# The first column pair of a SwiGLU block in seven products instead of eight, with the sum-free products of two pairs run first, fewer sum buffers, and the output projection in four parts instead of three

## The chip, the cores and the metric

The kernel runs on one core of a Trainium2 chip. The metric is the device time of one execution in microseconds (us). Before the change the median of three runs is 1446.42 us (1444.23 to 1446.85).

The engines are named as in the profile: PE (TensorE matmul; PEld its weight loads), DVE (VectorE), ACT (ScalarE), POOL (GpSimd) and SP, which only issues DMAs here. Each engine works through its own instruction queue in order. An instruction that has to wait for a semaphore holds up everything behind it on its engine.

## What is computed

Two layers of a hybrid decoder on 512 tokens of width 1024, in float32. Each layer has a token mixer, a cross-attention into 256 memory tokens and a SwiGLU feed-forward block, each followed by a residual and a LayerNorm. The change touches the feed-forward block:

```python
D_MODEL, SEQ, DEPTH, D_FF = 1024, 512, 2, 2816

def swiglu(x, w_in, w_out):
    g, u = jnp.split(x @ w_in, 2, axis=-1)
    return (jax.nn.silu(g) * u) @ w_out

def reference(...):
    h = layer_norm(x, ln0_g, ln0_b)
    for l in range(DEPTH):
        mix = hybrid_mixer(h, ...)
        h = layer_norm(DEEPNORM_ALPHA * h + mix, ln1_g[l], ln1_b[l])
        xa = memory_cross_attention(h, mem, ...)
        h = layer_norm(DEEPNORM_ALPHA * h + xa, ln2_g[l], ln2_b[l])
        ff = swiglu(h, w_ffn_in[l], w_ffn_out[l])
        h = layer_norm(DEEPNORM_ALPHA * h + ff, ln3_g[l], ln3_b[l])
    return h
```

## The kernel before

**Precision.** Every large product is made of three matmuls (`mm3`, lines 136 to 139): an operand is split into a rounded high part and the remainder, and high·high, high·low and low·high are added up in PSUM. The split (`split`, lines 100 to 102) is one copy on ACT (line 101, the high part) and one subtraction on DVE or POOL (line 102, the low part). A weight block of 128x1024 is loaded by SP into a staging buffer (`raw_...`, pool `stage`, 4 buffers), and its two halves are written into a ring of 4 slots (`w_...`, pool `ring`). A load waits until its staging buffer is free, and a split waits until its ring slot has been read for the last time by PE.

**The feed-forward block.** The 2816 gate columns and 2816 up columns are worked off in 11 pairs of column blocks (j = 0, 2, ... 20; each 256 columns of gate and 256 of up). The input x (tokens by features) is cut into four blocks: Bkt holds feature half k and token half t (B00, B10 of the first 256 tokens, B01, B11 of the last 256). A plain pair needs eight products of a 512x256 weight quarter by such a block. Ten of the eleven pairs use seven products (a scheme of Strassen's kind): some products take a sum of weight quarters, some take a sum of the blocks of x. A product is 24 matmuls of 128x256: 2 row blocks m, 4 slices k, 3 precision terms. So a plain pair is 192 matmuls (`swiglu_plain`, lines 348 to 371) and a pair in seven products 168 (`swiglu_seven`, lines 373 to 454).

**The sums of x.** T1 to T4, the sums of blocks, are made by `Quads` (lines 286 to 333). It is called as LN2, the LayerNorm ahead of the block, finishes each of the four 128-token tiles: PE transposes the tile (`lt_ln`, line 198), `take` (line 306) splits it into its Bkt block and updates the raw sums q11, q21 and q12. After tile 3, the last, `combine` (line 329) finishes T1 to T4, tile by tile. The first two products of a pair, on B00 and B10, need only tiles 0 and 1.

**The sums of weights.** A pair in seven products loads four quarters by SP: a11, a12, a22 into staging buffers and the fourth into s1, one of the quarter buffers (pool `quad`: 4 buffers, of which q11, q21, q12 take three while LN2 runs). DVE forms s3 = s1 + a11 and s2 = (s1 + a22) + a11 (lines 384 and 386), POOL issues two accumulating DMAs (`add_into`, line 284): s1 += a22, and later s2 += a12. Seven splits follow. A buffer that an accumulating DMA reads is free once that DMA has landed.

**Order.** The program's order per engine is set by a list scheduler at build time, from its own estimate of the durations. The plain pair j = 0 stands first: its 96 matmuls on B00 and B10 run while LN2 finishes tiles 2 and 3, and its 96 matmuls on B01 and B11 run while DVE and ACT make T1 to T4.

**The output projection** (`out_proj`, line 254) runs in three parts, after 4, 8 and 11 pairs (8, 8 and 6 row blocks of 128). Each part multiplies its row blocks by 128x1024 pieces of w_ffn_out, of which the first four take ring slots and the others `block` buffers, and adds the result to h by eight DVE instructions (line 273, two per token tile). In layer 0 the last part's tiles go straight into LN3, whose output is the input of layer 1's first projection (`pp_c`, weights `w_c`, split on ACT and POOL).

Of the kernel before, what the change touches and what calls it, by code (L numbers as in the profile page):

```python
# [20 lines left out]
P = 128  # L21
# [19 lines left out]
NBLK = 15  # L41
RAW = 4
TMP = 4
EVB = 6
# [7 lines left out]
def trunk(ctx: ExitStack, tc, a, out):  # L52
# [9 lines left out]
    quad = ctx.enter_context(tc.tile_pool(name="quad", bufs=4))  # L62
# [223 lines left out]
    class Quads:  # L286
# [4 lines left out]
        def __init__(self, name):  # L291
            self.name = name
            self.b = {(i, t): block([P, 2, 4, 256], F32R, f"B{i}{t}_{name}") for t in range(2) for i in range(2)}
            self.raw = {n: quarter([P, 4, 256], f"q{n}_{name}") for n in ("11", "21", "12")}
            self.d = {n: block([P, 2, 4, 256], F32R, f"{n}_{name}") for n in ("T3", "T1", "T2", "T4")}
            self.late = []

        def split_t(self, n, src, s, neg=False):
            hi, lo = self.d[n][:, 0, :, s], self.d[n][:, 1, :, s]
            if neg:  # L300
                ACT.activation(hi, src, AF.Copy, scale=-1.0)
                DVE.scalar_tensor_tensor(lo, src, -1.0, f(hi), ALU.mult, ALU.subtract)
            else:
                split(hi, lo, src)

        def take(self, i, tt, pv):
            s = slice((tt % 2) * P, (tt % 2 + 1) * P)
            b = self.b[i, tt // 2]
            r11, r21, r12 = (self.raw[n][:, :, s] for n in ("11", "21", "12"))
            split(b[:, 0, :, s], b[:, 1, :, s], pv)  # L310
            if tt < 2:
                ACT.activation((r11, r21)[i], pv, AF.Copy)
            elif i == 0:
                ACT.activation(r12, pv, AF.Copy)
                DVE.tensor_sub(r11, r11, pv)
                self.split_t("T1", r11, s)
            else:
                DVE.tensor_add(r11, r11, pv)
                DVE.tensor_sub(r12, pv, r12)

                def rest():
                    DVE.tensor_sub(r21, r11, r21)
                    self.split_t("T3", r12, s)
                    self.split_t("T2", r11, s, neg=True)
                    self.split_t("T4", r21, s)

                self.late.append(rest)
# [20 lines left out]
    def swiglu_plain(w, q, j, ph, pl, name):  # L348

        ws = [[split_quarter(load_quarter(w, kh, c0, f"g{c0}{kh}_{name}"), f"g{c0}{kh}_{name}") for kh in range(2)]  # L350
              for c0 in (j * P, DFF + j * P)]
        banks = [[bank(f"pp_f{j}{g}{m}_{name}") for m in range(2)] for g in range(2)]
        for t in range(2):
            for g in range(2):
                for kh in range(2):
                    for m in range(2):
                        ms = slice(m * P, (m + 1) * P)
                        for k in range(4):
                            mm3(banks[g][m][:, t * 256:(t + 1) * 256], ws[g][kh][:, 0, k, ms], ws[g][kh][:, 1, k, ms],
                                q.b[kh, t][:, 0, k, :], q.b[kh, t][:, 1, k, :],  # L360
                                kh == 0 and k == 0, kh == 1 and k == 3)
        out = []
        with tc.high_priority(offset=HP):
            for m in range(2):
                sg = tmp.tile([P, T], F32, tag="t", name=f"sg{j}{m}_{name}")
                ACT.activation(sg, banks[0][m], AF.Silu)
                DVE.tensor_mul(sg, sg, banks[1][m])
                split(ph[:, m, :], pl[:, m, :], sg)
                out.append((ph[:, m, :], pl[:, m, :]))
        return out  # L370

    def swiglu_seven(w, q, j, ph, pl, i0, name):
# [5 lines left out]
        s1, s2, s3 = (quarter([P, 1024], n(f"s{i}")) for i in range(1, 4))  # L378
        r11 = load_quarter(w, 0, cg, n("a11"))
        load_quarter(w, 0, cu, n("s1"), s1)  # L380
        r22 = load_quarter(w, 1, cu, n("a22"))
        r12 = load_quarter(w, 1, cg, n("a12"))
        w1 = split_quarter(r11, n("a11"))
        DVE.tensor_add(s3, s1, r11)
        add_into(s1, r22)
        DVE.tensor_add(s2, s1, r11)
        w7 = split_quarter(s3, n("s3"))
        w6 = split_quarter(s2, n("s2"))
        add_into(s2, r12)
        w2 = split_quarter(r12, n("a12"))  # L390
        w5 = split_quarter(s1, n("s1"))
        w3 = split_quarter(s2, n("s4"))
        w4 = split_quarter(r22, n("a22"))
        t3, t1, t2, t4 = q.t
# [23 lines left out]
        lo, hi = slice(0, 256), slice(256, 512)  # L418
# [4 lines left out]
        W = banks_of("fw", "cv")  # L423
        product(w7, t3, W, True, False)
# [3 lines left out]
        Y = banks_of("fy", "tr")  # L428
# [500 lines left out]
```

## Time and profile before

| | before |
|---|---|
| runs | 1444.23, 1446.42, 1446.85 us; median 1446.42 |
| the profiled execution | 1448.14 us, of which the span in the trace is 1446.4 |
| mean granted clock of PE | 0.992 |
| DMA | 168.62 MB, mean 117 GB/s |

The span is what the trace covers, from the first to the last instruction; 1.7 us of the profiled execution lie outside of it. In rows of the timeline the first two numbers are the start and the length in us, and what stands in brackets is the idle time of the engine just before and what ended it. A matmul row's length includes the way through the array, so the rate of matmuls is read from the distance of their starts. In rows of a window the columns are its length, then for each engine the busy time and the number of instructions, then the granted clock as a share of full speed, the DMA share and GB/s. The chain of waits lists what the end of a stretch hung on, piece by piece; a piece "DMA" is a transfer from its issue to its landing, and "issue" is time in which nothing is waited for that the profile shows.

### The profile page before, as it was taken

How to read it: one execution, taken by the hardware profiler on the slowest of the kernel's cores; microseconds unless marked ns; L12 is line 12 of the kernel's file. 1: busy time of each engine (PE TensorE's matmuls, PEld its weight loads, DVE VectorE, ACT ScalarE, POOL GpSimd, SP SyncE). 2: the span in 40 equal slices, each digit the busy share in tenths (PEclk: the TensorE clock that was granted, in tenths of full speed). 3: DMA queues.
4: the chain of work that ended last, by engine and by line, in shares of the span. 5: the costliest groups of instructions: out<-in, count | busy, mean ns of one | idle time of the engine just before them, and what ended most of it. 6: DMA issues, size and time to landing. Idle time of an engine off the chain costs nothing.

```text
span 1446.4 us, 22112 instructions
## 1 busy us (share of the span) xinstructions
PE 1405.3 (97%) x8943; PEld 1257.2 (87%) x8943; DVE 1015.9 (70%) x1674; ACT 608.8 (42%) x976; POOL 218.8 (15%) x124
## 2 busy tenths in 40 slices
PE   8999999999999999999979999999999999999997
PEld 7787878988999899899877888889889998998996
DVE  6699977557877367466859997685578664763767
ACT  5553362442555155245225335424424542561550
POOL 3467230000000000000133423300000000000000
PEclk9999999999999999999989999999999999999999
DMA  7423250221365265545242323612214662643641
GB/s 248 131 79 117 88 190 25 95 86 58 97 161 170 76 168 131 147 113 128 84 126 84 93 85 115 217 59 88 76 51 119 164 190 59 161 135 114 146 132 58
DMA packets 108730, 168.62 MB, mean 117 GB/s; under 512 B 7485, under 2 KB 81937, under 8 KB 108629
## 3 DMA queue, kind: packets, MB, share of 16 engines
q1 hardware_dynamic: 102548, 145.98, 32.1%
q0 software_dynamic: 5760, 20.97, 7.8%
q8 instruction: 70, 1.15, 0.3%
q14 instruction: 32, 0.25, 0.1%
q10 hardware_dynamic: 320, 0.27, 0.1%
HBM read 144.13 MB, written 2.10 MB: 101 GB/s over the span
## 4 chain that ended last, share of the span: by engine, by line
PE 76%; DVE 14%; DMA 5%; ACT 3%; issue 2%; POOL 0%; SPq 0%; DVEq 0%; POOLq 0%; ACTq 0%
DVE cv L590 6%; PE po_fo L137 5%; PE po_fo L138 5%; PE po_fo L139 5%; PE fx L402 5%; PE fx L404 5%; PE fx L403 5%; DMA s<-raw_a 3%; PE fw L404 2%; PE fw L403 2%; PE fw L402 2%; PE pp_xq L137 2%; PE pp_xq L138 2%; PE pp_xq L139 2%; PE po_mo L139 2%
## 5 line engine op out<-in xcount | busy, mean ns | idle before, releaser
L284 POOL DMA_DIRECT2D s<-raw_a x40 | 34.9, 885 | 873.4 <-DVE w_s L102 256.1
L590 DVE SCALAR_TENSOR_TENSOR cv<-u,chan,cv 128x511 f32<-128x511 f32 (+28 forms) x240 | 158.6, 728 | 0.3
L138 PE MATMUL po_fo<-w_fo,ph 128*128 128x512 f32 (+1 forms) x358 | 138.1, 386 | 0.0
L139 PE MATMUL po_fo<-w_fo,pl 128*128 128x512 f32 (+1 forms) x358 | 137.0, 386 | 0.0
L137 PE MATMUL po_fo<-w_fo,ph 128*128 128x512 f32 (+1 forms) x358 | 131.7, 386 | 0.0
L101 ACT ACTIVATE w_a<-raw_a 128x1024 fp32r<-128x1024 f32 x60 | 63.2, 1054 | 150.6 <-PE po_fo L139 124.6
L102 DVE TENSOR_TENSOR w_s<-s,w_s 128x1024 fp32r<-128x1024 f32 x80 | 97.3, 1220 | 33.3 <-ACT w_s L101 33.0
L101 ACT ACTIVATE w_s<-s 128x1024 fp32r<-128x1024 f32 x80 | 83.8, 1052 | 48.0 <-DMA s<-raw_a 27.6
L402 PE MATMUL fx<-T_ln,w_s 128*128 128x256 f32 x320 | 91.6, 287 | 3.5 <-ACT u L415 3.3
L403 PE MATMUL fx<-T_ln,w_s 128*128 128x256 f32 x320 | 91.2, 285 | 0.0
L404 PE MATMUL fx<-T_ln,w_s 128*128 128x256 f32 x320 | 90.6, 285 | 0.0
L273 DVE SCALAR_TENSOR_TENSOR h<-h,po_fo 128x512 f32<-128x512 f32 (+1 forms) x49 | 32.3, 671 | 71.2 <-PE po_fo L139 71.1
L102 DVE TENSOR_TENSOR w_a<-raw_a,w_a 128x1024 fp32r<-128x1024 f32 x60 | 73.0, 1220 | 9.1 <-ACT w_a L101 8.1
L139 PEld LDWEIGHTS po_fo<-w_fo,pl 128*128 128x128 f32 x358 | 67.3, 188 | 13.3
L138 PEld LDWEIGHTS po_fo<-w_fo,ph 128*128 128x128 f32 x358 | 67.3, 188 | 13.0
L137 PEld LDWEIGHTS po_fo<-w_fo,ph 128*128 128x128 f32 x358 | 66.9, 188 | 12.9
L402 PEld LDWEIGHTS fx<-T_ln,w_s 128*128 128x128 f32 x320 | 62.2, 194 | 4.2 <-ACT u L415 3.7
L102 DVE TENSOR_TENSOR w_fo<-raw_fo,w_fo 128x1024 fp32r<-128x1024 f32 x44 | 52.8, 1219 | 13.6 <-ACT w_fo L101 13.6
L403 PEld LDWEIGHTS fx<-T_ln,w_s 128*128 128x128 f32 x320 | 62.2, 194 | 0.0
L404 PEld LDWEIGHTS fx<-T_ln,w_s 128*128 128x128 f32 x320 | 61.8, 194 | 0.0
L138 PE MATMUL pp_xq<-hT_ln,w_xq 128*128 128x256 f32 (+1 forms) x192 | 61.3, 322 | 0.0
L139 PE MATMUL pp_xq<-hT_ln,w_xq 128*128 128x256 f32 (+1 forms) x192 | 60.3, 319 | 0.0
(315 smaller groups left out, 4478.3 us busy)
## 6 DMA issues: line engine op xcount, KB each, us to landing
raw_a<-w_ffn_in SPq DMA_DIRECT2D x60, 512.0 KB
raw_fo<-w_ffn_out SPq DMA_DIRECT2D x44, 512.0 KB
s<-raw_a POOLq DMA_DIRECT2D x40, 512.0 KB, 4.9
s<-w_ffn_in SPq DMA_DIRECT2D x20, 512.0 KB
raw_xk<-w_xkv SPq DMA_DIRECT2D x16, 512.0 KB
raw_c<-w_in SPq DMA_DIRECT2D x16, 512.0 KB
raw_xv<-w_xkv SPq DMA_DIRECT2D x16, 512.0 KB
raw_mo<-w_mix_out SPq DMA_DIRECT2D x16, 512.0 KB
```

The lines of the kernel that those rows point to most:

```text
L101: ACT.activation(hi, src, AF.Copy)
L102: eng.tensor_sub(lo, src, f(hi))
L137: PE.matmul(o, lh, rh, start=start, stop=False)
L138: PE.matmul(o, lh, rl, start=False, stop=False)
L139: PE.matmul(o, ll, rh, start=False, stop=stop)
L273: DVE.scalar_tensor_tensor(h[tt][:, c0:c1], h[tt][:, c0:c1], scale, bks[c][:, :c1 - c0], ALU.mult, ALU.add)
L284: POOL.dma_start(dst, src, accum_op=ALU.add)
L402: PE.matmul(o, wh, bh, start=start and k == 0, stop=False, skip_group_check=True)
L403: PE.matmul(o, wh, bl, start=False, stop=False, skip_group_check=True)
L404: PE.matmul(o, wl, bh, start=False, stop=stop and k == 3, skip_group_check=True)
L590: DVE.scalar_tensor_tensor(cv[ct][:, s:], u[:, ct, :T - s], wj, cv[ct][:, s:], ALU.mult, ALU.add)
```

## The change

`swiglu_plain` and `swiglu_seven` are replaced by one generator, `swiglu_pair`, for all 11 pairs. It first makes the two products that need no sum (X = a11·B00, Y = a12·B10) and then yields. For the first part of the output projection, pairs 0 and 2 are both started up to there, then `combine` is run, then the rest of pair 0 and of pair 2.

- The gate half of the first 256 tokens (`g`) is evicted right after Y into its own tile (pool `evp`, 6 to 8 buffers). Multiplying gate by up becomes four 128x256 DVE instructions per pair instead of two of 128x512.
- Weight sums are formed in place: a11 += s1 (DVE), s2 = a11 + a22 (DVE), s1 += a22 (POOL's accumulating DMA), a12 += s2 (another). Two quarter buffers per pair instead of three; the pools hold 5 quarters instead of 4, 5 staging buffers instead of 4, 14 blocks instead of 15.
- `Quads`: B01 is not stored any more. T1 is still made per tile; the three other sums are made in `combine` by whole 128x1024 instructions, after tile 3. They are now numbered T0 to T3 in the code: T0 is the old T2, T1 the old T3, T2 the old T1, T3 the old T4.
- The output projection has parts of 4, 6, 6 and 6 row blocks. In the last part of layer 0 only two of its weight pieces take ring slots.
- `reset`, a constant of the GLA scan, becomes a temporary tile that POOL fills in each layer.

```diff
-NBLK = 15
-RAW = 4
+NBLK = 14
+RAW = 5
-EVB = 6
+EVB = 8
...
-    quad = ctx.enter_context(tc.tile_pool(name="quad", bufs=4))
+    quad = ctx.enter_context(tc.tile_pool(name="quad", bufs=5))
...
-    def out_proj(w, stat, name, scale, norm=None, fin=False):
+    def out_proj(w, stat, name, scale, norm=None, fin=False, nring=RING):
-        wcs = [wchunk(w[k * P:(k + 1) * P, :], 1, D, f"{name}{k}", resident=k >= RING) for k in range(nk)]
+        wcs = [wchunk(w[k * P:(k + 1) * P, :], 1, D, f"{name}{k}", resident=k >= nring) for k in range(nk)]
...
         def combine(self):
-            for rest in self.late:
-                rest()
-            self.t = [self.d[n] for n in ("T3", "T1", "T2", "T4")]
+            t2, t4, t3 = (self.raw[n].rearrange("p k t -> p (k t)") for n in ("11", "21", "12"))
+            hi, lo = ([], [])
+            for i in (0, 1, 3):
+                d = self.new_t(i).rearrange("p j k t -> p j (k t)")
+                hi.append(d[:, 0])
+                lo.append(d[:, 1])
+            ACT.activation(hi[0], t2, AF.Copy, scale=-1.0)
+            DVE.scalar_tensor_tensor(lo[0], t2, -1.0, f(hi[0]), ALU.mult, ALU.subtract)
+            split(hi[1], lo[1], t3)
+            DVE.tensor_sub(t4, t2, t4)
+            split(hi[2], lo[2], t4)
...
-    def swiglu_plain(w, q, j, ph, pl, name):
...
-    def swiglu_seven(w, q, j, ph, pl, i0, name):
+    def swiglu_pair(w, q, j, pT, early, name):
...
+        r11 = load_quarter(w, 0, cg, n("a11"))
+        r12 = load_quarter(w, 1, cg, n("a12"))
+        w1 = split_quarter(r11, n("a11"))
+        w2 = split_quarter(r12, n("a12"))
         X = banks_of("fx", "acc")
         product(w1, q.b[0, 0], X, True, False)
         with tc.high_priority(offset=HP):
             x = copies("x")
+        Y = banks_of("fy", "cv" if early else "tr")
+        product(w2, q.b[1, 0], Y, True, True)
+        with tc.high_priority(offset=HP):
+            glo = two(evp, 256, "e", "g")
+            for m in range(2):
+                DVE.tensor_add(glo[m], Y[m][:, lo], x[m])
+                ACT.activation(glo[m], glo[m], AF.Silu)
+        yield
+        t2, t3, t1, t4 = q.t
+        s1, s2 = (quarter([P, 1024], n(f"s{i}")) for i in range(1, 3))
+        load_quarter(w, 0, cu, n("s1"), s1)
+        r22 = load_quarter(w, 1, cu, n("a22"))
+        DVE.tensor_add(r11, s1, r11)
+        DVE.tensor_add(s2, r11, r22)
+        add_into(s1, r22)
+        w6 = split_quarter(s2, n("s2"))
+        add_into(r12, s2)
+        w7 = split_quarter(r11, n("s3"))
+        w5 = split_quarter(s1, n("s1"))
+        w3 = split_quarter(r12, n("s4"))
+        w4 = split_quarter(r22, n("a22"))
         product(w6, t2, X, False, False)
...
-        quads.combine()
-        for part, (j0, nj) in enumerate(((0, 8), (8, 8), (16, 6))):
+        for part, (j0, nj) in enumerate(((0, 4), (4, 6), (10, 6), (16, 6))):
...
+            if part == 0:
+                next(pairs[0])
+                next(pairs[1])
+                quads.combine()
+            for pair in pairs:
+                for _ in pair:
+                    pass
```

In the built program PE has 48 matmuls fewer, DVE 68 instructions more, ACT 12 more, POOL 8 more, and SP as many as before. Three places show how the order moves. A name ends in numbers that only tell buffers apart; a line number of the program after is three less than the same helper's line before.

On DVE, at the end of LN2 in layer 0, `y_ln2_03` is the reciprocal deviation of tile 3, and `h3` is the tile itself, which PE transposes next. Before, the last steps stand between instructions on the blocks of x:

```order
L154 SCALAR_TENSOR_TENSOR t_ln2_03_3356<-y_ln2_03_3355,v_ln2_03_3351 128x1
L102 TENSOR_TENSOR T3_ln2_0_2982<-q12_ln2_0_2981,T3_ln2_0_2982 128x4x128
L159 SCALAR_TENSOR_TENSOR s_ln2_03_3357<-t_ln2_03_3356 128x1
L302 SCALAR_TENSOR_TENSOR T2_ln2_0_2984<-q11_ln2_0_2979,T2_ln2_0_2984 128x4x128
L160 SCALAR_TENSOR_TENSOR y_ln2_03_3355<-s_ln2_03_3357,y_ln2_03_3355 128x1
L102 TENSOR_TENSOR T4_ln2_0_2985<-q21_ln2_0_2980,T4_ln2_0_2985 128x4x128
L190 SCALAR_TENSOR_TENSOR h3_103<-h3_103,y_ln2_03_3355,gb_ln2_0_2972 128x512 x2
```

After the change the same place on DVE holds the weight sums and splits of pairs 0 and 2 (`raw_a112` is a11 of pair 2, `s12` its fourth quarter as loaded by SP, `s22` its s2):

```order
L99 TENSOR_TENSOR w_s20_0_3542<-s20_0_3535,w_s20_0_3542 128x1024
L99 TENSOR_TENSOR w_s10_0_3549<-s10_0_3534,w_s10_0_3549 128x1024
L99 TENSOR_TENSOR w_s40_0_3552<-raw_a120_0_3382,w_s40_0_3552 128x1024
L154 SCALAR_TENSOR_TENSOR y_ln2_03_3349<-t_ln2_03_3350,y_ln2_03_3349 128x1
L393 TENSOR_TENSOR raw_a112_0_3452<-s12_0_3706,raw_a112_0_3452 128x1024
L151 SCALAR_TENSOR_TENSOR t_ln2_03_3350<-y_ln2_03_3349,v_ln2_03_3345 128x1
L394 TENSOR_TENSOR s22_0_3707<-raw_a112_0_3452,raw_a222_0_3709 128x1024
L156 SCALAR_TENSOR_TENSOR s_ln2_03_3351<-t_ln2_03_3350 128x1
L157 SCALAR_TENSOR_TENSOR y_ln2_03_3349<-s_ln2_03_3351,y_ln2_03_3349 128x1
L187 SCALAR_TENSOR_TENSOR h3_100<-h3_100,y_ln2_03_3349,gb_ln2_0_2972 128x512 x2
```

The finishing of tile 3 now stands behind the sums of pair 2 (L393 and L394). The quarter buffer into which SP loads `s12` is that of `s20`, pair 0's s2; the load waits in SP's queue for POOL's accumulating DMA raw_a120 += s20, which reads `s20`, and for the split w_s20. Layer 1 has the same order.

On PE, around the transposes of tile 3 (`lt_ln2_03`), before:

```order
L139 MATMUL pp_f011_0_3425<-B10_ln2_0_2976,w_g28161_0_3419 128x256
L198 MATMUL lt_ln2_03_0_3365<-ident_85,h3_103 128x128 x4
L198 MATMUL lt_ln2_03_1_3377<-ident_85,h3_103 128x128 x4
L137 MATMUL pp_f000_0_3422<-B01_ln2_0_2977,w_g00_0_3404 128x256
L137 MATMUL pp_f001_0_3423<-B01_ln2_0_2977,w_g00_0_3404 128x256
```

The same place on PE after:

```order
L359 MATMUL fy12_0_3493<-B10_ln2_0_2976,w_a122_0_3459 128x256
L195 MATMUL lt_ln2_03_0_3359<-ident_85,h3_100 128x128 x4
L195 MATMUL lt_ln2_03_1_3369<-ident_85,h3_100 128x128 x4
L357 MATMUL fx00_0_3390<-T0_ln2_0_3524,w_s20_0_3542 128x256
L357 MATMUL fx10_0_3391<-T0_ln2_0_3524,w_s20_0_3542 128x256
```

In both, 96 matmuls on B00 and B10 stand ahead of the transposes. Behind them came matmuls on B01, a copy of the transposed tile; now come matmuls on T0, a sum made by `combine`.

On ACT, at the end of layer 0, `w_c0_100` to `w_c0_111` are the first four weight pieces of layer 1's first projection, and `hT00_ln3` is the split of LN3's transposed tiles. Before:

```order
L101 ACTIVATE hT00_ln3_0_6547<-lt_ln3_00_0_6640 128x4x128
L101 ACTIVATE hT01_ln3_0_6548<-lt_ln3_00_1_6648 128x4x128
L101 ACTIVATE w_c0_100_6903<-raw_c0_100_6901 128x1024
L101 ACTIVATE w_c0_101_6908<-raw_c0_101_6906 128x1024
L101 ACTIVATE w_c0_110_6915<-raw_c0_110_6913 128x1024
L101 ACTIVATE hT00_ln3_0_6547<-lt_ln3_01_0_6714 128x4x128
L101 ACTIVATE hT01_ln3_0_6548<-lt_ln3_01_1_6722 128x4x128
L101 ACTIVATE w_c0_111_6920<-raw_c0_111_6918 128x1024
```

The same place on ACT after:

```order
L98 ACTIVATE w_c0_100_6954<-raw_c0_100_6952 128x1024
L98 ACTIVATE w_c0_101_6959<-raw_c0_101_6957 128x1024
L98 ACTIVATE wa_1_7281<-wa_raw_1_7273 128x8x16
L578 ACTIVATE w2_555<-wa_raw_1_7273 96x256
L98 ACTIVATE hT00_ln3_0_6598<-lt_ln3_00_0_6691 128x4x128
L98 ACTIVATE hT01_ln3_0_6599<-lt_ln3_00_1_6699 128x4x128
L98 ACTIVATE w_c0_110_6966<-raw_c0_110_6964 128x1024
L98 ACTIVATE w_c0_111_6971<-raw_c0_111_6969 128x1024
```

The first two pieces now stand ahead of LN3's first tile, since their ring slots are those of the last pair's weights and no longer those of the output projection. POOL makes the low halves of all four in the same sequence, and each waits for its ACT copy. The other two still wait for the last token tile of the output projection.

More of the change, by code (lines that the diff above doesn't have):

```diff
@@ L346, in split_quarter @@
         return w
[L348 to L372 removed]
+    def swiglu_pair(w, q, j, pT, early, name):
         n = lambda s: f"{s}{j}_{name}"
         cg, cu = j * P, DFF + j * P
[L378 to L394, printed above, removed]
+        lo, hi = slice(0, 256), slice(256, 512)
         def product(wq, b, banks, start, stop):
```

75 lines of the change are left out of this document (28 added, 47 removed).

## The prediction

> **What bounds the kernel now.** I began with the busy time of each engine and the chain that ended last (sections 1 and 4 of the page).
>
> ```profile
> PE 1405.3 (97%) x8943; PEld 1257.2 (87%) x8943; DVE 1015.9 (70%) x1674; ACT 608.8 (42%) x976; POOL 218.8 (15%) x124
> PE 76%; DVE 14%; DMA 5%; ACT 3%; issue 2%; POOL 0%; SPq 0%; DVEq 0%; POOLq 0%; ACTq 0%
> ```
>
> PE is busy for 97% of the span, so a matmul taken away is time gained, and a new hole in PE is time lost. Hence the question at each place: does PE still have something to do? The timeline of the end of LN2 in layer 0 (first five rows), and of the first stall behind it in each layer:
>
> ```profile
> 371.13 0.28 PE L137 MATMUL pp_f<-B_ln,w_g 128*128 128x256 f32 x1
> 371.25 0.28 PE L138 MATMUL pp_f<-B_ln,w_g 128*128 128x256 f32 x1
> ...
> 382.52 0.29 PE L139 MATMUL pp_f<-B_ln,w_g 128*128 128x256 f32 x1
> 382.65 1.04 PE L198 MATMUL lt_ln<-ident,h 128*128 128x128 f32 x8
> 383.93 0.74 PE L137 MATMUL pp_f<-B_ln,w_g 128*128 128x256 f32 x4 [0.25 <-ACT B_ln L101]
> ...
> 430.48 0.39 PE L402 MATMUL fx<-T_ln,w_s 128*128 128x256 f32 x1 [1.50 <-ACT u L415]
> ...
> 1145.31 0.39 PE L402 MATMUL fx<-T_ln,w_s 128*128 128x256 f32 x1 [1.82 <-ACT u L415]
> ```
>
> Matmuls of 128x256 start 0.12 us apart. The 96 on B00 and B10 run from 371.13 to 382.65; exactly then tile 3's transposes start, and 0.25 us after them PE goes on with the plain pair. The same end of LN2 on DVE, and how a DVE queue looks when it does wait for an accumulating DMA, 18 us later:
>
> ```profile
> 381.24 1.40 DVE L190 SCALAR_TENSOR_TENSOR h<-h,y_ln,gb_ln 128x512 f32<-128x512 f32 x2
> ...
> 399.43 1.23 DVE L386 TENSOR_TENSOR s<-s,raw_a 128x1024 f32<-128x1024 f32 x1 [1.71 <-DMA s<-raw_a]
> ```
>
> Tile 3 is finished at 381.24 plus 0.7 (its first half), in step with PE.
>
> **The change part by part.** The windows give what PE loses now in the stretches that change: the starts of both feed-forward blocks (rows 1 and 4) and the passage between the layers (rows 2 and 3).
>
> ```profile
> 383.00:436.00 53.00, 50.73 (x411) 49.35 (x410) 40.33 (x50) 30.58 (x49) 4.50 (x5) 1.00 0.56 137
> 712.00:732.00 20.00, 11.97 (x60) 9.64 (x59) 19.90 (x28) 6.19 (x8) 9.36 (x4) 0.86 0.31 76
> 732.00:760.00 28.00, 28.00 (x219) 27.58 (x218) 10.02 (x24) 9.43 (x14) 7.21 (x3) 0.92 0.37 118
> 1097.50:1150.00 52.50, 49.97 (x392) 48.57 (x390) 39.22 (x48) 29.18 (x47) 4.37 (x5) 0.97 0.55 133
> ```
>
> *Removed.* 24 matmuls per layer at 0.12: 2.9 us each. PE idles 53.00 - 50.73 = 2.3 us at layer 0's start, and at layer 1's 52.50 - 49.97 = 2.5 plus 0.03 x 52.5 = 1.6 of lowered clock, 4.1. These small holes belong to the old order; I count all of them as gone, which favours the change.
>
> *New wait ahead of tile 3.* This is the largest term. Tile 3's last DVE steps now stand behind a11 += s1 and s2 = a11 + a22 of pair 2. These need the quarter s12, which SP can load only once POOL's accumulating DMA has read pair 0's s2. So an accumulating DMA and a load, one after the other, stand between pair 0's s2 and the transposes. The pieces of the chain of waits price them:
>
> ```profile
> 394.15 0.54 issue
> ...
> 394.71 4.70 DMA s<-raw_a
> ...
> 404.74 6.11 DMA s<-raw_a
> 414.79 6.46 DMA raw_a<-w_ffn_in
> ...
> 1086.82 6.58 DMA s<-w_ffn_in
> 1108.90 4.63 DMA s<-raw_a
> 1129.29 4.77 DMA raw_a<-w_ffn_in
> 1135.44 8.40 DMA s<-raw_a
> ```
>
> The groups give the sums and splits (mean ns of one behind the busy time), and three timeline rows the smaller steps:
>
> ```profile
> L102 DVE TENSOR_TENSOR w_s<-s,w_s 128x1024 fp32r<-128x1024 f32 x80 | 97.3, 1220 | 33.3 <-ACT w_s L101 33.0
> L386 DVE TENSOR_TENSOR s<-s,raw_a 128x1024 f32<-128x1024 f32 x20 | 24.4, 1222 | 47.2 <-DMA s<-raw_a 47.2
> L101 ACT ACTIVATE w_s<-s 128x1024 fp32r<-128x1024 f32 x80 | 83.8, 1052 | 48.0 <-DMA s<-raw_a 27.6
> ...
> 368.53 3.48 DVE L102 TENSOR_TENSOR w_g<-raw_g,w_g 128x1024 fp32r<-128x1024 f32 x3
> ...
> 383.28 1.08 ACT L101 ACTIVATE B_ln<-lt_ln 128x512 fp32r<-128x512 f32 x2 [3.00 <-PE lt_ln L198]
> ...
> 431.33 0.42 DVE L433 TENSOR_TENSOR sg<-fy,x 128x256 f32<-128x256 f32 x1
> ```
>
> When is pair 0's s2 ready? At 371.13 PE starts the early products as before. DVE ends its splits of early weights near 372, as it does now (368.53 + 3.48), and has then six steps of tile width (0.6 to 0.7 each, the row at 381.24 halved), one sum of 1.2, a 128x256 step of 0.4 and less than 0.1 of small ones; with s2 itself some 377.8 if each starts a little before the one ahead of it ends, as such rows do. Then 0.5 us to issue, the accumulating DMA 4.6 to 6.1 (once 8.4), the load 4.8 to 6.6, two sums at 1.2, four small steps and half of tile 3, 3.4 together. That gives 391.1 to 394.4; with 8.4 for the DMA 396.7. PE has run out at 382.65. The middle, 5.4 for the DMA and 5.6 for the load, gives 392.7 and **10 us of idle PE per layer**. A load that overlaps nothing could be some quicker, so I take 7.5 as the lower bound and 14 as the upper. Queued behind the waiting sum on DVE are not only tile 3 but all of `combine`, which feeds the next matmul of PE. Nothing on PE covers it: pair 2's early products are already in the 96.
>
> *Combine in the open.* Before, 96 matmuls on B01 and B11 (11.5 us) lay over it. Now the matmul behind the transposes reads T0. From their start: transposes of one half 0.5, ACT's copy of q12 0.6 (row at 383.28, halved), a DVE difference 0.6, ACT's high part of T2 0.6, its low part and the second half's sum on DVE 1.2, ACT's high part of T0 at 128x1024 1.05, DVE's q21 half over it and then T0's low part 1.2, which the second matmul of each triple needs: 6.5 us, less 1.0 in which PE transposes. I take **5.4 us per layer** (4.5 to 7).
>
> *Clock.* After long waits the clock drops. The passage between the layers shows it: waits of 3.77 and 4.01 us, and behind them 28 us at 0.92, so 0.08 x 28 = 2.2 us lost. The new wait is longer than these. **2.2 us per layer** (1.6, as at layer 1's start, to 3.5, if the hole between transposes and combine lowers it twice).
>
> The Trainium skill, "TensorE: Matmul & The Clock Gate", section "What's actually happening", says that the clock halves after an idle window of about 3.4 us and returns after a busy one as long. By that a wait costs 1.7 us, and the sum would be 1 us lower over both layers. The trace agrees for the passage between the layers but not for layer 1's start, where a wait of only 1.82 us went with a lowered clock.
>
> *Output projection in four parts.* Eight more additions to h per layer (0.7 us each on DVE) lie beside PE, which is the fuller engine (50.7 against 40.3 us in the first window above). Pair 4's first weights, however, split only when the projection's last half tile frees a ring slot, and with four row blocks this half tile lasts 12 matmuls:
>
> ```profile
> 455.84 0.23 PE po_fo L138
> 456.07 0.23 PE po_fo L139
> ```
>
> 12 x 0.23 = 2.8 us, of which 0.7 pass before the slot is free. ACT's 1.05 and DVE's 1.2 end 0.2 to 1.5 us late; I take **0.7 us per layer**. The parts of six last 4.1 us and hide it.
>
> *Rest of the block.* The split multiplication (0.42 twice, as at 431.33, in place of one of 0.7), `reset` on POOL, the larger pools: cost 0, covered by PE's matmuls. If the cover failed on DVE, two more small steps per pair would cost at most 0.2 us x 11.
>
> *Passage between the layers.* Two of the four POOL splits of `w_c` move ahead of LN3. The rows of LN3's tile 2:
>
> ```profile
> 713.06 0.15 DVE L160 SCALAR_TENSOR_TENSOR y_ln<-s_ln,y_ln 128x1 f32<-128x1 f32 x1
> ...
> 719.31 7.01 POOL L102 TENSOR_TENSOR w_c<-raw_c,w_c 128x1024 fp32r<-128x1024 f32 x3 [49.04 <-DVE hT_ln L102]
> 719.86 1.86 DVE L157 SCALAR_TENSOR_TENSOR y_ln<-t_ln,y_ln 128x1 f32<-128x1 f32 x1
> 721.76 2.28 DVE L154 SCALAR_TENSOR_TENSOR t_ln<-y_ln,v_ln 128x1 f32<-128x1 f32 x1
> 724.07 2.27 DVE L159 SCALAR_TENSOR_TENSOR s_ln<-t_ln 128x1 f32<-128x1 f32 x1
> 726.65 2.34 POOL L102 TENSOR_TENSOR w_c<-raw_c,w_c 128x1024 fp32r<-128x1024 f32 x1 [0.33 <-ACT w_c L101]
> 726.86 2.15 DVE L160 SCALAR_TENSOR_TENSOR y_ln<-s_ln,y_ln 128x1 f32<-128x1 f32 x1
> 726.99 0.58 PE L137 MATMUL pp_c<-hT_ln,w_c 128*128 128x256 f32 x1 [3.77 <-DVE h L273]
> 731.58 1.12 PE L198 MATMUL lt_ln<-ident,h 128*128 128x128 f32 x4 [4.01 <-DVE hT_ln L102]
> ```
>
> DVE steps on one column, 0.15 us elsewhere, take 1.9 to 2.3 while POOL splits, four of them one after the other, and PE waits 7.8 us. With two splits left, two stretched steps go: 2 x 2.1 = 4.2, and some of the clock loss, 0.8. **Gain 5 us**, between 0 (the two left over stretch as many steps) and 10 (both waits and 2.2 of clock go).
>
> The Trainium skill, "SBUF — State Buffer", section "SBUF: two separate sides", says that DVE and POOL share a port pair that one instruction holds to its end. The stretched steps, each near POOL's 2.34, agree; by it the gain is one step's stretch per split moved, the same 4.
>
> *Sum* against the profiled execution, 1448.1 us: layer 0 +10 +5.4 +2.2 +0.7 -2.9 -2.3 = +13.1; layer 1 +10 +5.4 +2.2 +0.7 -2.9 -4.1 = +11.3; passage -5; together +19.4, so 1467.5. The profiled execution lies 1.7 above the median of the runs; set on the median, 1446.4, the forecast is **1466**.
>
> **The rivals.** With w for the wait ahead of tile 3 the sum is 1445.8 + 2w.
>
> *A, as above*: w from 7.5 to 14, 1456 to 1478 with the other bounds. For it speak the order of the queues and that no accumulating DMA shown took less than 4.63 us.
>
> *B, a short wait*: the load finds idle DMA engines and lands soon, or pair 0's s2 is ready several us before 377.8. w from 1 to 4, 1448 to 1454. Against it: even 4.63 + 4.77 behind 377.8 reach 387.
>
> *C, faster*: the matmuls removed and the passage decide. If both waits between the layers go (10 instead of 5), the time is 1440.8 + 2w, below the old median as long as w stays under 2.8, about 1442 at w near 0.5. For that s12 would have to land at about 380, 2 us behind the sum that frees its buffer. Against it speak both DMA rows; for it only that the scheduler saw no wait there.
>
> *D, longer still*: DVE, kept for 8 us or so at pair 2's sums, owes the splits of the output projection's first part; PE catches up with it and waits again at w_fo or at pair 4, 4 to 8 us per layer, 1474 to 1485. For it: DVE has only 12.7 us of slack in the 53 of the first window. Against: a part's loads start early.
>
> That the matmuls would not go away is excluded by the order.
>
> **How the numbers follow.** A 0.55, B 0.17, C 0.13, D 0.15. Time 1466. The range goes from C's upper end to most of D, 1443 to 1482, which leaves out under 2 in 10. What can be told from no change is about 0.2%, 2.9 us: below 1443.5 lies C, 0.13; within 1443.5 to 1449.3 the part of B with w up to 1.7, 0.07; above A, D and the rest of B, 0.80.
>
> **What would show it.** Right: in the new trace, a gap of PE of 8 to 12 us just ahead of the transposes `lt_ln` of tile 3, DVE's sum a11 += s1 waiting there for the DMA s<-w_ffn_in; a second gap near 5 us between these transposes and the first fx on T, put down to DVE or ACT on T; lowered clock behind them; all this twice. In the passage, POOL's splits two by two and fewer stretched steps. Wrong: transposes at 383 to 385; or PE gaps at pair 4 of more than 2 us (D); or the passage unchanged.

## The result and the profile after

| | before | after |
|---|---|---|
| median of the runs, us | 1445.53 (1444.23 to 1446.85, 4 runs) | 1468.66 (1468.38 to 1470.22, 4 runs) |
| profiled execution, and its span | 1448.14, 1446.4 | 1470.22, 1468.2 |
| mean granted clock of PE | 0.992 | 0.983 |

The changed kernel takes 1.0162 times as long (95% interval 1.0145 to 1.018), 23 us more. The forecast was 1466, slower by 20.

The page after begins with the busy time of each engine (share of the span, instructions) and the shares of the chain that ended last:

```profile
PE 1407.8 (96%) x8895; PEld 1256.8 (86%) x8895; DVE 1037.0 (71%) x1742; ACT 615.5 (42%) x988; POOL 222.1 (15%) x132
PE 74%; DVE 16%; issue 3%; ACT 3%; DMA 3%; SPq 0%; POOL 0%; DVEq 0%; ACTq 0%; POOLq 0%
```

PE executes 48 matmuls fewer and is yet busy 2.5 us longer: part of them ran at a lower clock, as the timeline below shows. DVE's share of the chain grows from 14 to 16%, that of DMA falls from 5 to 3%. PE's waits in the new trace, by what ended them (us in total, times, longest):

```profile
PE lt_ln L195 <- DVE h L187: 15.8, 2, 8.1
PE fx L357 <- ACT T_ln L323: 7.6, 2, 3.8
...
PE pp_xq L134 <- DVE h L270: 2.1, 2, 1.1
PE pp_c L134 <- DVE h L270: 1.9, 1, 1.9
...
PE pp_xq L134 <- ACT hT_ln L98: 1.4, 2, 0.7
```

The first two are new: 11.5 us per layer at the start of the feed-forward block, ahead of tile 3's transposes and between these and the first matmul on T0. In PE's timeline of layer 0, with three of the matmuls behind them:

```profile
393.09 1.94 PE L195 MATMUL lt_ln<-ident,h 128*128 128x128 f32 x8 [7.71 <-DVE h L187]
398.85 0.79 PE L357 MATMUL fx<-T_ln,w_s 128*128 128x256 f32 x2 [3.82 <-ACT T_ln L323]
...
401.01 0.42 PE L359 MATMUL fx<-T_ln,w_s 128*128 128x256 f32 x1
401.23 0.42 PE L357 MATMUL fx<-T_ln,w_s 128*128 128x256 f32 x1
401.44 0.41 PE L358 MATMUL fx<-T_ln,w_s 128*128 128x256 f32 x1
```

The eight transposes take 1.94 us (1.04 before), and the matmuls start 0.21 apart where 0.12 is usual: PE comes out of the gap at about half its clock.

To see where the 21.8 us of the span arise, I compared when PE reaches the same place in both traces:

| place | before | after | shift |
|---|---|---|---|
| layer 0, first output projection (`po_mo`) | 203.11 | 201.91 | -1.2 |
| second output projection (`po_xo`) | 321.05 | 323.64 | +2.6 |
| first product of the feed-forward block | 371.13 | 373.72 | +2.6 |
| LN3's first transposes | 715.89 | 729.41 | +13.5 |
| layer 1, `po_mo` | 918.05 | 927.25 | +9.2 |
| `po_xo` | 1035.40 | 1047.80 | +12.4 |
| first product of the feed-forward block | 1085.51 | 1097.86 | +12.35 |
| end of the span | 1446.4 | 1468.2 | +21.8 |

A stretch costs the difference of two shifts: the feed-forward blocks +10.9 and +9.45, the stretch from LN3 into layer 1's mixer -4.3, and, where I had put nothing, the stretch from `po_mo` to `po_xo` +3.8 and +3.2. That one holds LN1 and the query projection of the cross-attention (`pp_xq`), which the change's text does not touch.

**What holds tile 3.** DVE's timeline from pair 0's last splits to tile 3's last step:

```profile
383.15 1.22 DVE L99 TENSOR_TENSOR w_s<-s,w_s 128x1024 fp32r<-128x1024 f32 x1
384.28 1.22 DVE L99 TENSOR_TENSOR w_s<-raw_a,w_s 128x1024 fp32r<-128x1024 f32 x1
...
385.88 1.22 DVE L99 TENSOR_TENSOR w_s<-s,w_s 128x1024 fp32r<-128x1024 f32 x1
...
387.35 1.22 DVE L99 TENSOR_TENSOR w_s<-raw_a,w_s 128x1024 fp32r<-128x1024 f32 x1
...
389.16 1.23 DVE L393 TENSOR_TENSOR raw_a<-s,raw_a 128x1024 f32<-128x1024 f32 x1 [0.53 <-DMA s<-w_ffn_in]
...
390.67 1.23 DVE L394 TENSOR_TENSOR s<-raw_a,raw_a 128x1024 f32<-128x1024 f32 x1 [0.15 <-DMA raw_a<-w_ffn_in]
...
392.19 1.42 DVE L187 SCALAR_TENSOR_TENSOR h<-h,y_ln,gb_ln 128x512 f32<-128x512 f32 x2
```

and in the table of windows PE's last full stretch and the gap (length; busy us and instructions of PE, PEld, DVE, ACT, POOL; clock, DMA share, GB/s):

```profile
373.70:385.50 11.80, 11.69 (x97) 11.46 (x95) 11.80 (x20) 7.43 (x13) 1.88 (x2) 1.00 0.47 89
385.50:393.00 7.50, 0.00 (x0) 0.00 (x0) 6.75 (x14) 1.78 (x3) 1.37 (x2) 0.79 0.73 226
```

DVE is busy for every one of the 11.80 us in which PE has matmuls, and for 6.75 of the 7.50 in which PE has none. For the load of s12, which I expected it to wait for, it waits 0.53 us, and 0.15 for another, that of pair 2's a22. The chain of waits names a DMA all the same:

```profile
385.97 4.61 DMA raw_a<-w_ffn_in
...
390.67 1.23 DVE s L394
...
392.19 0.76 DVE h L187
...
393.09 1.95 PE lt_ln L195 x8
```

It follows whatever ended last, and that is the load of a22 by 0.15 us. Beside it ran DVE's own queue, and so did the path that I had priced. POOL issues the accumulating DMA a12 += s2 of pair 0, and SP the load of s12 once that DMA has landed:

```profile
380.89 0.87 POOL L281 DMA_DIRECT2D raw_a<-s  x1 [2.03 <-DVE v_ln L177]
```

```profile
385.51 0.37 SPq L332 DMA_DIRECT2D s<-w_ffn_in  x1
```

DVE has s12 at 389.16. So the queue and the transfers ended almost together. Which of them sets the gap, this trace can't tell; for that I moved the work.

### The profile page after: what moved, and what is told of

Read it like the earlier page. It is cut to its first block, busy times and chain, and to the rows that moved or that the text cites. A ratio compares the mean times of both kernels' runs of the same rounds, so it can differ in the third digit from the quotient of the medians.

```text
span 1468.2 us, 22156 instructions
## 1 busy us (share of the span) xinstructions
PE 1407.8 (96%) x8895; PEld 1256.8 (86%) x8895; DVE 1037.0 (71%) x1742; ACT 615.5 (42%) x988; POOL 222.1 (15%) x132
## 4 chain that ended last, share of the span: by engine, by line
PE 74%; DVE 16%; issue 3%; ACT 3%; DMA 3%; SPq 0%; POOL 0%; DVEq 0%; ACTq 0%; POOLq 0%
DVE cv L563 5%; PE fx L358 5%; PE fx L359 5%; PE fx L357 5%; PE po_fo L134 4%; PE po_fo L135 4%; PE po_fo L136 4%; PE fw L357 3%; PE fw L359 3%; PE fw L358 3%; PE pp_xq L135 2%; PE pp_xq L136 2%; PE pp_xq L134 2%; PE po_xo L136 2%; PE po_xo L135 2%
## 5 line engine op out<-in xcount | busy, mean ns | idle before, releaser
L281 POOL DMA_DIRECT2D s<-raw_a x22 | 19.2, 875 | 870.4 <-DVE mv_ln L175 334.5
L135 PE MATMUL po_fo<-w_fo,p 128*128 128x512 f32 (+1 forms) x358 | 136.6, 386 | 0.0
L136 PE MATMUL po_fo<-w_fo,p 128*128 128x512 f32 (+1 forms) x358 | 135.4, 386 | 0.0
L134 PE MATMUL po_fo<-w_fo,p 128*128 128x512 f32 (+1 forms) x358 | 129.4, 387 | 0.0
L98 ACT ACTIVATE w_a<-raw_a 128x1024 fp32r<-128x1024 f32 x66 | 67.7, 1053 | 142.4 <-issue 107.5
L270 DVE SCALAR_TENSOR_TENSOR h<-h,po_fo 128x512 f32<-128x512 f32 (+1 forms) x65 | 42.8, 676 | 102.0 <-PE po_fo L136 102.0
L99 DVE TENSOR_TENSOR w_a<-raw_a,w_a 128x1024 fp32r<-128x1024 f32 x66 | 79.5, 1222 | 45.8 <-ACT w_a L98 45.7
L357 PE MATMUL fx<-T_ln,w_s 128*128 128x256 f32 x352 | 101.4, 290 | 7.9 <-ACT T_ln L323 7.6
L358 PE MATMUL fx<-T_ln,w_s 128*128 128x256 f32 x352 | 101.3, 289 | 0.1
L359 PE MATMUL fx<-T_ln,w_s 128*128 128x256 f32 x352 | 100.2, 288 | 0.2
L136 PEld LDWEIGHTS po_fo<-w_fo,p 128*128 128x128 f32 x358 | 67.3, 188 | 13.3
L135 PEld LDWEIGHTS po_fo<-w_fo,p 128*128 128x128 f32 x358 | 67.3, 188 | 12.8
L134 PEld LDWEIGHTS po_fo<-w_fo,p 128*128 128x128 f32 x358 | 66.8, 188 | 13.3 <-DVE h L270 0.6
L357 PEld LDWEIGHTS fx<-T_ln,w_s 128*128 128x128 f32 x352 | 69.1, 197 | 9.4 <-ACT T_ln L323 8.4
L358 PEld LDWEIGHTS fx<-T_ln,w_s 128*128 128x128 f32 x352 | 69.2, 197 | 0.7 <-DVE T_ln L324 0.7
L359 PEld LDWEIGHTS fx<-T_ln,w_s 128*128 128x128 f32 x352 | 68.8, 197 | 0.6 <-DVE w_s L99 0.6
L99 DVE TENSOR_TENSOR w_s<-raw_a,w_s 128x1024 fp32r<-128x1024 f32 x44 | 53.8, 1222 | 17.8 <-ACT w_s L98 17.8
L134 PE MATMUL pp_xq<-hT_ln,w_xq 128*128 128x256 f32 (+1 forms) x192 | 61.2, 324 | 3.5 <-DVE h L270 2.1
L135 PE MATMUL pp_xq<-hT_ln,w_xq 128*128 128x256 f32 (+1 forms) x192 | 62.2, 325 | 0.0
L136 PE MATMUL pp_xq<-hT_ln,w_xq 128*128 128x256 f32 (+1 forms) x192 | 61.4, 321 | 0.0
```

The costliest lines, as they stand in the source:

```text
L98: ACT.activation(hi, src, AF.Copy)
L99: eng.tensor_sub(lo, src, f(hi))
L134: PE.matmul(o, lh, rh, start=start, stop=False)
L135: PE.matmul(o, lh, rl, start=False, stop=False)
L136: PE.matmul(o, ll, rh, start=False, stop=stop)
L270: DVE.scalar_tensor_tensor(h[tt][:, c0:c1], h[tt][:, c0:c1], scale, bks[c][:, :c1 - c0], ALU.mult, ALU.add)
```

## The experiments

Ratios are against the kernel before, run beside them on the same chip (median 1445.05 for the first four, 1444.18 for the others).

### 1. Only pair 2's sums behind tile 3

```diff
-        DVE.tensor_add(r11, s1, r11)
-        DVE.tensor_add(s2, r11, r22)
+        with tc.issue_after(late[0]) if early and j == 2 else nullcontext():
+            DVE.tensor_add(r11, s1, r11)
+            DVE.tensor_add(s2, r11, r22)
```

`late[0]` is the last DVE step on LN2's tile 3 (L187 after), `issue_after` puts an instruction behind it in the queue. This takes the DMAs out of tile 3's path and leaves the splits there.

> The changed kernel with one order edge: pair 2's two weight sums on DVE stand behind the last step of LN2's tile 3. Theory 1, as in the prediction: these two sums and the DMAs that they wait for are the first gap of PE (7.7 and 8.1 us), so nearly all of it goes: about 15 us and some clock less than the changed kernel's 1468.7, near 1451. Theory 2, from the changed kernel's timeline: DVE is at work there all the time and waits for a DMA for only 0.7 us; four splits of pair 0's weights still stand ahead of tile 3, so the gap shrinks by 3 us in each layer, and the two sums then fall into combine and give 1 to 2.5 back: 1464 to 1467.

Measured: 1466.86 (1465.64 to 1467.26), 1.0148 (1.0131 to 1.0165). PE's waits:

```profile
PE lt_ln L197 <- DVE h L189: 9.6, 2, 4.8
PE fx L359 <- ACT T_ln L325: 9.4, 2, 4.7
```

DVE waits for no DMA ahead of tile 3 any more, and PE still waits 4.8 us: DVE's other work holds up tile 3 for some three fifths of the gap by itself. The 2.9 that go are about the two sums themselves (2 x 1.13) and the 0.53 + 0.15 of waiting. Of these 2.9, 0.9 come back in the second wait, since the sums now stand in the middle of `combine`. The theory that DVE's wait for the DMAs is the whole cost (1451) falls.

### 2. Pair 0's splits behind tile 3 as well

```diff
+        with tc.issue_after(late[2]) if early and j == 2 else nullcontext():
             DVE.tensor_add(r11, s1, r11)
             DVE.tensor_add(s2, r11, r22)
...
+        with tc.issue_after(late[0]) if early else nullcontext():
             w6 = split_quarter(s2, n("s2"))
         add_into(r12, s2)
+        with tc.issue_after(late[1]) if early else nullcontext():
             w7 = split_quarter(r11, n("s3"))
...
```

The last line stands for all four further splits; `late[1]` and `late[2]` are the low parts of T1 and T3 in `combine`.

> The changed kernel with order edges: pair 0's first split of a sum behind tile 3's last step, its other splits behind the low part of T1, pair 2's two sums behind the low part of T3. Theory 2: DVE has no work on weights ahead of tile 3 any more, PE's first gap falls from 8 to under 1 us in each layer, the second gap (3.8) stays, and with the shorter wait 1 to 2 us of lowered clock go in each layer: 1449 to 1453. Theory 1: the same as the run with the two sums alone moved, within 2 us.

Measured: 1456.72 (1454.61 to 1457.13), 1.0078 (1.0063 to 1.0093). PE's timeline:

```profile
386.30 0.63 PE L197 MATMUL lt_ln<-ident,h 128*128 128x128 f32 x4 [1.00 <-DVE h L189]
...
392.13 0.80 PE L361 MATMUL fx<-T_ln,w_s 128*128 128x256 f32 x2 [4.21 <-ACT T_ln L325]
```

The first gap is down from 7.71 to 1.00, and 0.37 between the transposes, and the kernel 12 us faster than after: the splits, the sums and what the sums waited for were nearly all of the gap. It came out some 4 us above the upper end of my expectation. The second gap has grown by 0.4, and behind it PE's matmuls start 0.21 apart until 397.1, about as long as in after; of the lowered clock only the transposes' part went.

### 3. `combine` by tile, as before

```diff
+                def rest():
+                    ...
+                    ACT.activation(t0[0], r11, AF.Copy, scale=-1.0)
+                    DVE.scalar_tensor_tensor(t0[1], r11, -1.0, f(t0[0]), ALU.mult, ALU.subtract)
+                    split(t1[0], t1[1], r12)
+                    DVE.tensor_sub(r21, r11, r21)
+                    split(t3[0], t3[1], r21)
+                self.late.append(rest)
         def combine(self):
...
+            for rest in self.late:
+                rest()
```

> The changed kernel with combine by token tiles again, as before the change, in place of whole 128x1024 instructions after tile 3. If the whole instructions cost PE the second gap's length: that gap falls from 3.8 to about 2.6 and the time to about 1466. Theory 2: the halves for tile 2 (four DVE steps of 0.6) are then more work ahead of tile 3 on a DVE that is already full, the first gap grows by 1.7 to 2.4, and the time is 1469 to 1471.

Measured: 1469.97 (1469.41 to 1472.05), 1.0175 (1.016 to 1.019), no better than after. PE's waits:

```profile
PE lt_ln L195 <- DVE h L187: 18.5, 2, 9.3
...
PE fx L362 <- ACT T_ln L321: 6.8, 2, 3.4
```

The second gap gives up 0.4, since tiles 0 to 2 are done earlier; but done on the same full DVE, so the first grows by 1.4.

### 4. LN1's block given back

The pool `block` has 14 buffers in place of 15. ACT's timeline before, and then after, at LN1 of layer 0:

```profile
241.62 0.60 ACT L101 ACTIVATE hT_ln<-lt_ln 128x512 fp32r<-128x512 f32 x1 [6.20 <-PE lt_ln L198]
```

```profile
244.61 2.96 ACT L98 ACTIVATE w_xq<-raw_xq 128x1024 fp32r<-128x1024 f32 x3 [10.35 <-PE po_mo L136]
...
247.47 0.58 ACT L98 ACTIVATE hT_ln<-lt_ln 128x512 fp32r<-128x512 f32 x1
```

ACT makes the high part of the first half tile as early as before (234.82 before, 233.67 after); its second split, shown here, now comes behind three splits of `w_xq`, 5.85 us later. What is missing is a place for the first half tile's low part (`hT10`). DVE's rows before and after:

```profile
235.45 0.69 DVE L102 TENSOR_TENSOR hT_ln<-lt_ln,hT_ln 128x512 fp32r<-128x512 f32 x1
```

```profile
247.45 0.67 DVE L99 TENSOR_TENSOR hT_ln<-lt_ln,hT_ln 128x512 fp32r<-128x512 f32 x1
```

It comes 12 us later, during the last matmuls of `po_mo`, which still read `block` buffers. That these set its block free fits the times; the trace does not name the buffer. In this kernel `hT10` goes into two quarter buffers that lie idle at that time:

```diff
+        hT[1][0] = [quad.tile([P, 2, T], F32R, tag="s", name=f"hT10{x}_{name}") for x in range(2)]
...
-        hT = new_hT(n_("ln1"))
+        hT = new_hT(n_("ln1"), True)
```

> The changed kernel with one block of LN1's output (hT10) in two quarter buffers, which are idle there, so that LN1 has as many blocks as before the change. Theory: the pool of 14 blocks in place of 15 holds up the first split of LN1's output, reorders the projection behind it and costs 3.8 us in layer 0 and 3.2 in layer 1 (gaps of 0.7, 1.1 and 0.2 us and a lowered clock): 1461 to 1463. Rival, that these gaps come from the weight loads that a fifth staging buffer sends earlier: no change, 1467 to 1470.

Measured: 1463.10 (1461.48 to 1465.75), 1.0127 (1.0111 to 1.0143): 5.6 less than after. The stretch from `po_mo` to `po_xo` takes 117.81 us in layer 0, against 117.94 before and 121.73 after, and of PE's waits at `pp_xq` one of 0.2 us is left in layer 0.

### 5. One block held in the kernel before

The same from the other side: the kernel before, with one of its 15 blocks taken over LN1.

```diff
+        held = block([P, 8], F32, n_("held"))
+        POOL.memset(held, 1.0)
         hT = new_hT(n_("ln1"))
...
         mov = mov_hT(hT)
+        ACT.activation(junk[:, :8], h[3][:, :8], AF.Identity, bias=held[:, 0:1])
```

> The kernel before with one of its 15 blocks held from ahead of LN1 until behind it (a tile that POOL fills and ACT reads), so that LN1 has 14 as in the changed kernel. Theory: the same order of LN1 and of the projection behind it as in the changed kernel, and its cost: 3.5 us in each layer, 1450 to 1453. Rival, that the cost hung on the fifth staging buffer: 1444 to 1447.

Measured: 1450.71 (1448.04 to 1453.02), 1.0039 (1.0026 to 1.0052). PE's timeline of this kernel, then of after:

```profile
250.37 0.62 PE L137 MATMUL pp_xq<-hT_ln,w_xq 128*128 128x256 f32 x3 [0.69 <-ACT hT_ln L101]
...
252.74 0.39 PE L137 MATMUL pp_xq<-hT_ln,w_xq 128*128 128x256 f32 x1 [1.07 <-DVE h L273]
```

```profile
250.41 0.61 PE L134 MATMUL pp_xq<-hT_ln,w_xq 128*128 128x256 f32 x3 [0.69 <-ACT hT_ln L98]
...
252.78 0.38 PE L134 MATMUL pp_xq<-hT_ln,w_xq 128*128 128x256 f32 x1 [1.07 <-DVE h L270]
```

The same two gaps to the hundredth. Holding one block costs 1450.71 - 1444.18 = 6.5 us over two layers and giving it back saves 5.6, so this cost is shown from both sides. It does not hang on the fifth staging buffer, since this kernel has four. In its profiled execution the stretches from `po_mo` to `po_xo` are 2.5 and 2.4 us longer than before, less than the 3.8 and 3.2 of after: in layer 0 the clock does not fall behind the two gaps here (the last section comes back to this).

### 6. Splits behind tile 3 and LN1's block together

The edits of 2 and 4 in one kernel.

> The changed kernel with both repairs: pair 0's splits and pair 2's sums behind tile 3, and LN1's block back. If the two costs lie in different places and add up: 12.0 and 5.6 us off the changed kernel's 1468.7, 1450 to 1452. It stays above the kernel before, since the second gap (4.2 us in each layer and the lowered clock) is left.

Measured: 1450.14 (1447.35 to 1451.18), 1.0037 (1.0026 to 1.0048). The two costs add up: 11.7 above the kernel before in experiment 2, 6.0 here. The rest is read from its windows in layer 0:

```profile
371.00:386.00 15.00, 9.43 (x75) 8.81 (x74) 13.87 (x29) 10.12 (x16) 1.87 (x2) 0.94 0.48 105
386.00:400.00 14.00, 13.82 (x95) 13.23 (x95) 12.40 (x13) 6.14 (x10) 1.74 (x2) 0.82 0.63 175
```

PE idles 5.6 + 0.2 us here and 0.7 later in the block. The clock columns also count time in which PE had nothing to do, so its loss is read from the starts: from 385.71 to 391.02 some 20 matmuls take 0.21 each where 0.12 is usual, 1.9 us, and 0.9 more passes between the first five of them, hidden in the lengths of their rows. That is 9.3, less 2.9 for the matmuls saved and 2.3 for the old holes, +4.1. From the first product to LN3 this kernel takes 4.35 us more than before (349.11 against 344.76). So even without the first gap, `combine` in the open and the clock behind it cost more than 24 matmuls bring.

### 7. Only the ring slots of the last output projection, in the kernel before

```diff
+                     nring=2 if part == 2 and l < L - 1 else RING)
```

> The kernel before with one part of the change alone: in layer 0's last output projection only two weight pieces take ring slots, so two of the next projection's splits move ahead of LN3. Theory: this part of the change alone gains what the passage between the layers gained in the changed kernel (5.4 us): 1439 to 1441, the two PE waits of 3.8 and 4.0 us together 4 us shorter. Rival, that the gain in the changed kernel came from its shorter last part or its pools: 1444 to 1446.

Measured: 1439.72 (1434.77 to 1442.99, 9 runs), 0.9965 (0.9951 to 0.9979). This part of the change gains 4.5 us by itself, and the kernel is the fastest of all that were run. PE's waits in the passage fall from 7.8 to 3.6 us, and its clock from 712 to 732 us is 1.00 in place of 0.86. POOL's and DVE's timelines in the passage between the layers:

```profile
717.88 5.74 POOL L102 TENSOR_TENSOR w_c<-raw_c,w_c 128x1024 fp32r<-128x1024 f32 x2 [12.96 <-DVE h L273]
```

```profile
717.85 3.57 DVE L184 SCALAR_TENSOR_TENSOR h<-h,mv_ln,gb_ln 128x512 f32<-128x512 f32 x2
```

Two POOL splits stand here in place of three and one. Beside them a pair of wide DVE steps takes 3.57 us, where the same pair takes 1.40 in before, ahead of POOL's splits (start 715.95).

### 8. No ring slot at all there

```diff
+                     nring=0 if part == 2 and l < L - 1 else RING)
```

> The same with no weight piece in a ring slot: all four splits on POOL move ahead of LN3's tiles. If DVE's one-column steps are stretched only while POOL splits, none is stretched beside LN3 any more and both PE waits go: 3 to 5 us less than with two pieces, 1435 to 1438. If the waits are DVE's own work in LN3, no more than 1 us less: 1438 to 1441.

Measured: 1443.49 (1440.57 to 1445.4), 0.9986 (0.9977 to 0.9996), a miss. POOL's, DVE's and PE's timelines:

```profile
703.86 8.02 POOL L102 TENSOR_TENSOR w_c<-raw_c,w_c 128x1024 fp32r<-128x1024 f32 x3 [2.00 <-ACT w_c L101]
```

```profile
705.98 3.63 DVE L184 SCALAR_TENSOR_TENSOR h<-h,mv_ln,gb_ln 128x512 f32<-128x512 f32 x2
```

```profile
690.21 0.51 PE L138 MATMUL po_fo<-w_fo,ph 128*128 128x512 f32 x1 [0.93 <-DVE w_fo L102]
...
728.77 0.66 PE L198 MATMUL lt_ln<-ident,h 128*128 128x128 f32 x4 [2.26 <-DVE hT_ln L102]
```

POOL's splits leave LN3's tile 2 and meet its earlier tiles, whose wide DVE steps they stretch instead; PE still waits 2.26 for LN3 and newly 0.93 for a weight piece of the projection itself. These waits are only 1.3 us more than with two pieces, and the kernel is 3.8 slower; where the rest arises was not followed up. Of four, two and no ring slots, two is best.

## Why the prediction came out right, and where its steps were wrong

**Direction and size.** 1466 was forecast and 1468.66 measured, inside A (1456 to 1478). This agreement is partly luck: by the span, the two feed-forward blocks cost 20.35 where I had 24.4, and 7.0 us at LN1 that I had not seen make up for it.

**First gap: right place, nearly right size, only half the reason.** 10 us were forecast, 7.5 as the lower bound; 7.71 and 8.12 were measured. I followed the transfers alone: accumulating DMA, load, two sums. The four splits of pair 0 (4 x 1.13 from start to start, 4.5 us) stood ahead of tile 3, three of them in the rows that I had quoted, and I gave them no term. Since they ran while the transfers were under way, the total still fits. With the splits in place the transfers add little: without transfers and sums 4.8 of 7.7 stayed (experiment 1), and with the splits gone too, 1.0 (experiment 2). Counting DVE's work would have shown the rest: in the 11.8 us that were to cover it, DVE had no free time at all. The difference between 10 and 7.7 is mostly the load. Pair 0's s2 was ready 6.5 us behind the first product (I had 6.7) and the accumulating DMA took 4.6 from its issue (5.4), but the load only 3.65, from 385.51 to 389.16, where I had 5.6 and 4.8 as its least.

**Combine in the open.** 5.4 forecast; the gap that the trace shows is 3.82 in both layers, below my bounds of 4.5 to 7, but it is not the whole cost. DVE's low part of T0:

```profile
399.36 1.22 DVE L324 SCALAR_TENSOR_TENSOR T_ln<-q_ln,T_ln 128x1024 fp32r<-128x1024 f32 x1
```

It ends at 400.58, 7.5 us behind the start of the transposes. I had 6.5, and even that was more than my terms as listed, which give 5.75, or 6.4 with DVE's q21 half counted in full. But PE did not wait for it: with the high parts there it ran the four matmuls that need nothing else. From 398.85 to 401.01 only five matmuls start, 1.07 us of work at 0.21 each, so some 1.1 us are lost that the rows' lengths hide for the most part. With them `combine` cost about 4.9, near the forecast, by another way than I had drawn up: steps that took longer, PE starting before the last of them, and transposes that took 0.9 longer at the low clock and so shortened the gap.

**Clock.** 2.2 per layer forecast, somewhat too small. In layer 0 PE idles 7.71 + 3.82 + 0.15 at the start and, by the windows behind it, 0.7 later in the block, 12.4; less 2.3 and 2.9 this makes +7.2, and the block took +10.9. The 3.7 left is in part the waits just named that the rows hide, 1.1 less the 0.15 already counted. The rest is the clock. The starts give it directly: the transposes lose 0.9, and 17 matmuls that start 0.21 apart in place of 0.12 lose 1.6, together 2.5. In layer 1 the low clock covers some 28 matmuls, and with the transposes the loss is 3.5, my upper bound. The windows behind both gaps of layer 0 show the same:

```profile
393.00:399.00 6.00, 2.09 (x9) 1.72 (x9) 4.57 (x7) 2.98 (x5) 0.37 (x1) 0.50 0.82 154
399.00:404.00 5.00, 4.80 (x21) 4.22 (x22) 3.85 (x4) 2.08 (x3) 0.00 (x0) 0.54 0.35 104
404.00:412.00 8.00, 8.00 (x69) 8.00 (x69) 3.42 (x5) 4.11 (x6) 0.00 (x0) 1.00 0.22 68
```

**Ring slot at pair 4.** 0.7 forecast, 0.20 measured:

```profile
468.23 0.39 PE L357 MATMUL fx<-B_ln,w_a 128*128 128x256 f32 x1 [0.20 <-ACT w_a L98]
```

**Passage.** Right: -5 forecast; the shift falls by 5.4 up to `pc`, the projection behind LN3 and `pp_c` (746.42 before, 754.52 after), and the mechanism alone gives 4.5 in experiment 7. POOL's splits came two by two, and of the four stretched one-column steps two are left:

```profile
733.59 1.66 DVE L151 SCALAR_TENSOR_TENSOR t_ln<-y_ln,v_ln 128x1 f32<-128x1 f32 x1
...
735.77 1.79 DVE L154 SCALAR_TENSOR_TENSOR y_ln<-t_ln,y_ln 128x1 f32<-128x1 f32 x1
```

**The step that failed.** "The larger pools: cost 0", under the rest of the block. I looked at the pools that grew and not at the one that shrank, `block`, 15 to 14, whose users are spread over the whole layer. It costs 5.6 to 6.5 us, at LN1, in both layers (experiments 4 and 5).

**Rivals.** B and C needed a short first gap, and C both passage waits gone; neither came. D's further waits at w_fo and pair 4 did not come; from 404 us to LN3 PE waits 0.21 twice and the 0.20 above, no more.

**What stays open.** Moving pair 0's splits and leaving pair 2's sums was not tried; as the load of s12 waits for the accumulating DMA and arrives at 389.16 even so, little might be gained by it, and the splits and the transfers may each be enough for most of the gap. What the lowered clock costs was read from the starts of the matmuls; no run took it away alone. That `combine` could be covered by matmuls on a stored B01, as before, was not tried with the new order: it needs the buffer that the change gave up.

## What to carry to other kernels

When work is moved ahead to cover a wait, add up all that then stands in the queue of the engine that has to end the wait; the chain of waits names only the last of two paths that end together. A pool that loses a buffer costs time at the place where its lifetimes are tightest, often far from the edit, so list every user of it. And take a bundled change apart: here one line of it gained 4.5 us by itself, and the rest lost some 28.

## What the runs showed of the hardware

A gap costs more than its own length, as the 2.5 and 3.5 us of lost clock above show. Behind the second gap in layer 1 (3.82 us, up to 1123.42) the clock stays low for longer than in layer 0:

```profile
1124.00:1136.00 12.00, 11.80 (x73) 11.30 (x73) 6.20 (x7) 4.42 (x7) 0.00 (x0) 0.72 0.25 87
```

If PE runs at half clock first and then at full, 0.72 over 12 us means 0.28 x 12 / 0.5 = 6.7 us at half, up to 1130.7, and PE's matmuls do start 0.21 apart until 1130.5, 7.1 us behind the first matmul on T0. In layer 0 the 0.54 between 399 and 404 us puts the return at 403.6, 4.7 us behind the first matmul on T0. The Trainium skill, "TensorE: Matmul & The Clock Gate", section "What's actually happening", has full clock return after at least one busy window of about 3.4 us, and says that the windows run freely, whenever the work starts. An estimate by that page is 3.4 to 6.8 us. The 4.7 us of layer 0 lie within it; the 7.1 of layer 1 do not, unless the first matmuls, with waits between them, do not count as busy, which no run here shows.

The clock can also be low behind short waits: at LN1, behind gaps of 0.69 and 1.07 us, the window is at 0.83, where the kernel before has 1.00 at the same time:

```profile
254.00:262.00 8.00, 8.00 (x60) 8.00 (x59) 6.30 (x16) 1.79 (x3) 0.00 (x0) 0.83 0.23 79
```

That window alone is 0.17 x 8 = 1.4 us of lost clock, more than either gap. But it need not be: behind two gaps of 0.7 and 1.1 us in layer 1 of the same trace it stays at 1.00 (975 to 990 us), and with the gaps of layer 0 in the kernel of experiment 5 the window from 254 to 262 us is at 1.00 too and holds 68 matmuls in place of 60. In the kernel before, the wait of 1.50 us at 430.48 leaves the clock at 1.00 (430.3 to 436 us), while behind that of 1.82 at 1145.31 it is 0.66 (1145 to 1150 us). The length of a short gap alone does not tell.

And the contention of DVE and POOL, known from one-column steps before (0.15 to some 2 us), also holds for wide ones: a pair of 128x512 took 3.57 and 3.63 us beside POOL's splits, 1.40 without them. POOL's work is not free where DVE carries the path.
